# A one-core decoder layer: the token table laid out by rank, the norm passes moved behind the last low part, and the output projection's constants loaded on the pool queue

## The chip, the cores and the metric

The kernel runs on one core of a Trainium2 chip. The metric is the device time of one execution in microseconds; lower is better. A core has a matrix engine (TensorE, PE in the profile), VectorE (DVE), ScalarE (ACT), GpSimd (POOL) and SyncE (SP). Each engine works its own instructions off in order and waits for others through semaphores. DMAs are issued from the queues of SP, ACT and POOL; an issue stands in its engine's order like any other instruction, and what uses the data waits until it has landed.

## The reference

One layer over 2048 tokens of width 1024, in float32. First a mixer: one projection of the input feeds sliding-window attention, a gated linear recurrence (HGRN2) and cross-attention to 256 memory tokens; their outputs go through one output projection. Then a mixture of 16 experts of which each token uses two. Each half ends in a layer norm of a scaled residual.

```python
proj = x @ w_in[l] + b_in[l]
...
mix = jnp.concatenate([swa_with_sinks(...), hgrn2(...), memory_attention(...)], axis=-1)
x = layer_norm(ALPHA * x + mix @ w_out[l], ln1_g[l], ln1_b[l])
x = layer_norm(ALPHA * x + moe(x, w_router, router_bias, w_gate[l], w_up[l], w_down[l]), ln2_g[l], ln2_b[l])
```

The router takes, of four groups of four experts, the group whose two best scores have the largest sum, and the two best experts in it:

```python
scores = jax.nn.sigmoid((x2 @ w_router).astype(jnp.float32))
sel = scores + router_bias.astype(jnp.float32)
grouped = sel.reshape(-1, N_GROUPS, EXPERTS_PER_GROUP)
group_score = jnp.sum(lax.top_k(grouped, TOP_K)[0], axis=-1)
best = jnp.argmax(group_score, axis=-1)
...
h = jax.nn.silu(xb @ w_gate[e]) * (xb @ w_up[e])
return h @ w_down[e]
```

## The kernel before

**Precision.** Every large product is three products of rounded parts: a high part (`AF.Copy` into float32r on ScalarE) and a low part (the rest, a subtraction on VectorE) of each factor; high by high, high by low and low by high are summed (`matmul3_steps`, line 63). So each operand tile costs one ScalarE and one VectorE pass. In what follows, the split of a tile is this pair.

**Order of the work.** TensorE's instructions run in program order (`manual_schedule`). For the other engines a planner orders the instructions ahead of time: it simulates the kernel and, when an engine is free, takes the earliest in program order of those that it holds ready. `tc.issue_after` keeps an instruction behind another in that order; `hold` makes a DMA wait for another instruction. On the chip each engine then follows the planned order, whatever is ready.

**Stages.** Attention, then the recurrence (`hgrn_phase`), then the output projection with first layer norm and router (`outproj_phase`), then the experts (`moe_phase`).

**Output projection.** It goes over 16 blocks of 128 tokens. `load_mix` brings the mixer's output back from DRAM (`mixT`, written from the tile `hmix` at line 900) and splits it (lines 944 and 945). `layer_norm` normalises a block with ln1's constants `g1` and `b1`; the result goes to DRAM twice, as `x1` and as the start of the sum `z`. `g1`, `b1`, the router's weights `wr` and its bias `rb` are loaded at the head of the phase on ScalarE's queue (lines 1045 to 1054). `route_block` chooses two experts per token, some forty small VectorE operations. `rank_block` counts, by a product with a triangle of ones, how many earlier tokens chose the same expert (the rank), and scatters a pair (token, weight) of 8 bytes into a DRAM table, at row `expert * 2304 + rank`. There are two such tables, `T[0]` for the first and `T[1]` for the second choice; a row is filled in one of them only, and `fill_tables` sets all the rest to a large number in the recurrence.

**Into the experts.** `plan_slots` sorts the experts by their count of tokens: slot 0 has the fullest expert and room for 336 tokens, slots 10 to 15 have room for 256 (`CAPS`). `fetch` loads slot 0's rows of both tables (line 1500) and takes the smaller (line 1502); the token list `ig` drives the gather of the rows of `x1` into `xg` (`gathered`, line 1491). `fetch_all` loads all slots' rows of both tables in six DMAs of 8-byte elements on ScalarE's queue (line 1516), takes the smaller, and picks each slot's expert by a product with a one-hot and a sum (lines 1517 to 1530). `early` (line 1769) is a copy of slot 0's weights for `keep_warm`, twelve products whose result nobody uses, which TensorE does while it waits; then come slot 0's transposes (line 1543) and their splits (line 1545, tile `xt`).

**A slot.** `gemm1` goes over four column groups `j` of the expert's width. In each it loads and splits gate and up weights (lines 1621, 1629 and 1630), multiplies (tile `ph`), takes silu on ScalarE (1635), the product with up on VectorE (1640), and splits the result into `h` (1651 and 1652; the last line is the low part). The down weights are split in between (1606 and 1607). `gemm2` multiplies `h` by the down weights (line 1688, tile `py`) with the transposes of the next slot's tokens interleaved, scales by the router's weight, and adds the rows into `z` in DRAM (line 1725).

**The second layer norm.** As soon as a block of tokens is complete (`READY` says how many blocks are after each slot), `bring` gathers its rows of `z` (line 1563, tile `zt`). `scale` takes the statistics (`bn_stats` at 1572, `bn_aggr` at 1574) and the root, by `pow` on POOL (1582). `write` makes two VectorE passes over the block, 1586 and 1587, the first of which subtracts the mean and multiplies by `g2`, the second multiplies by the root and adds `b2`. `put` stores it (1592). `beside(j)` places these in the next slot's `gemm1`: `scale` after the first column group, `write` and `put` after the second; the last column group's product waits for the passes (`passed`). The blocks of slots 9 to 15 are 2, 1, 2, 1, 2, 2 and 2. Three more blocks follow in the ending, beside the last slot's `gemm2`; the last slot's own rows are finished where they are (1700 and 1701), and the ending takes roots by `Ln` and `Exp` on ScalarE (1578 and 1579).

A last part, for tokens that fit no slot (`plan_over`), is run only if a slot overflows.

## Time and profile before

| | us |
|---|---|
| median of 3 runs | 1642.01 |
| the three runs | 1643.66, 1642.01, 1641.55 |
| the profiled execution | 1645.28 |
| its span, first to last instruction | 1643.7 |

| engine | busy us | share of the span |
|---|---|---|
| TensorE products (PE) | 1512.4 | 92% |
| TensorE weight loads (PEld) | 1354.3 | 82% |
| VectorE (DVE) | 1144.8 | 70% |
| ScalarE (ACT) | 824.3 | 50% |
| GpSimd (POOL) | 548.7 | 33% |

A timeline row gives the start and the length in microseconds, engine, source line, operation, output and inputs, shapes, count, and in brackets how long the engine had been idle and what ended that. A `q` after the engine marks its queue, as in an issue of a DMA. A row of waits gives who waited for whom, the sum, how many times, and the longest. A row of a group gives busy time and mean ns of one. A row by stretches gives the stretch and its length, then busy time of PE, PEld, DVE, ACT and POOL with the count of instructions, then TensorE's granted clock as a share of full speed, the mean busy share of the 16 DMA engines, and GB/s. The granted clock over the whole span is 0.974.

### The profile page before, as it was taken

To read this page: it belongs to the slowest core of one execution; us is meant where nothing else is said; L and a number is where in the kernel's file an instruction comes from. 1 tells how busy PE (TensorE), PEld (TensorE's weight loads), DVE (VectorE), ACT (ScalarE), POOL (GpSimd) and SP (SyncE) were. 2 spreads that over 40 slices of the span, in tenths; PEclk is the share of its full clock that TensorE was granted. 3 is DMA by queue.
4 is the path that set the end of the run, shared out by engine and by line. 5 is a ranking of instruction groups with operands and counts; after the bars stand their busy time and mean duration, and the time that the engine had idled before them with its cause. 6 is when DMAs were issued, how large, how long until landed. Compare 5 with 4: busy or idle time off the path is not lost. (4 is left out here: it accounts for less than half of the span.)

```text
span 1643.7 us, 28391 instructions
## 1 busy us (share of the span) xinstructions
PE 1512.4 (92%) x10293; PEld 1354.3 (82%) x10293; DVE 1144.8 (70%) x2724; ACT 824.3 (50%) x1840; POOL 548.7 (33%) x723
## 2 busy tenths in 40 slices
PE   8899999978999998989999299999999999999994
PEld 7899999977899997767777188988888888989883
DVE  5688888897677678668888465554555556666667
ACT  4576776766344445343332154545555554545544
POOL 3233333465745554123333211111111124232342
PEclk9999999999999999999999699999999999999997
DMA  9422222341222222364331787777777778889872
GB/s 275 159 91 97 97 97 97 110 147 52 93 76 66 65 66 90 97 213 167 142 142 78 156 242 196 181 195 208 207 206 194 207 221 238 255 248 272 228 223 100
DMA packets 241580, 258.66 MB, mean 157 GB/s; under 512 B 26224, under 2 KB 191249, under 8 KB 241436
## 3 DMA queue, kind: packets, MB, share of 16 engines
q1 hardware_dynamic: 203216, 182.03, 35.4%
q0 software_dynamic: 21088, 69.86, 15.6%
q10 hardware_dynamic: 17132, 4.91, 1.4%
q8 instruction: 83, 1.36, 0.4%
q14 instruction: 61, 0.50, 0.1%
HBM read 189.32 MB, written 69.01 MB: 157 GB/s over the span
## 5 line engine op out<-in xcount | busy, mean ns | idle before, releaser
L63 PEld LDWEIGHTS ph<-xt,w 128*128 128x128 f32 x3072 | 394.9, 188 | 5.6 <-DVE w L1630 3.8
L63 PE MATMUL ph<-xt,w 128*128 128x256 f32 (+8 forms) x3072 | 397.1, 291 | 2.5 <-DVE w L1630 2.5
L63 PE MATMUL pj<-xt,w 128*128 128x256 f32 x2016 | 290.3, 288 | 10.0 <-DVE xt L139 4.0
L63 PEld LDWEIGHTS pj<-xt,w 128*128 128x128 f32 x2016 | 259.2, 191 | 15.9 <-DVE xt L139 5.4
L1688 PE MATMUL py<-w,h 128*128 128x512 f32 (+8 forms) x936 | 244.2, 406 | 13.3 <-DVE h L1652 12.2
L1630 DVE TENSOR_TENSOR w<-raw,w 128x1024 fp32r<-128x1024 f32 x128 | 153.2, 1221 | 85.7 <-ACT w L1629 85.5
L1688 PEld LDWEIGHTS py<-w,h 128*128 128x128 f32 (+8 forms) x936 | 161.7, 181 | 58.6 <-DVE h L1652 14.7
L63 PE MATMUL py<-w,xt 128*128 128x512 f32 x672 | 174.2, 408 | 6.8 <-ACT xt L944 6.8
L1725 POOL DMA_INDIRECT zd<-z,ioall x37 | 57.3, 1550 | 322.3 <-ACT xt L1545 213.9
L1629 ACT ACTIVATE w<-raw 128x1024 fp32r<-128x1024 f32 x128 | 132.3, 1053 | 59.9 <-PE ph L63 42.9
L63 PEld LDWEIGHTS py<-w,xt 128*128 128x128 f32 x672 | 123.7, 192 | 34.9 <-ACT xt L944 7.3
L1545 DVE TENSOR_TENSOR xt<-tr,xt 128x512 fp32r<-128x512 f32 (+8 forms) x84 | 50.3, 599 | 124.6 <-ACT xt L1545 124.4
L63 PE MATMUL pj<-w,xt 128*128 128x512 f32 x336 | 89.2, 405 | 0.0
L339 POOL TENSOR_SCALAR prob<-prob,den 128x128 f32<-128x128 f32 x128 | 45.8, 376 | 107.8 <-ACT prob L382 57.9
L1545 ACT ACTIVATE xt<-tr 128x512 fp32r<-128x512 f32 (+8 forms) x84 | 43.7, 521 | 70.1 <-PE tr L1543 70.1
L1635 ACT ACTIVATE sl<-ph 128x256 f32<-128x256 f32 (+8 forms) x64 | 25.7, 402 | 98.4 <-PE ph L63 98.4
L1607 DVE TENSOR_TENSOR w<-raw,w 128x2048 fp32r<-128x2048 f32 x32 | 73.2, 2288 | 0.0
L814 DVE COPY_PREDICATED A<-mask,pl 128x512 f32<-128x512 uint8 x56 | 50.3, 899 | 32.5 <-PE pl L812 31.5
L1239 POOL DMA_INDIRECT T<-row,dst x32 | 34.1, 1067 | 111.6 <-DVE dst L1237 95.3
L63 PEld LDWEIGHTS pj<-w,xt 128*128 128x128 f32 x336 | 60.6, 191 | 10.6
L1703 ACT ACTIVATE z<-py,tball 128x512 f32<-128x512 f32 x56 | 38.5, 688 | 55.2 <-PE py L1688 53.8
L1592 POOL DMA_INDIRECT out<-zt,fin x15 | 39.1, 2606 | 67.5 <-DVE zt L1587 65.7
(388 smaller groups left out, 2880.5 us busy)
## 6 DMA issues: line engine op xcount, KB each, us to landing
raw<-in_w_gate SPq DMA_DIRECT2D x64, 512.0 KB, 4.9
raw<-in_w_up SPq DMA_DIRECT2D x64, 512.0 KB, 5.8
raw<-in_w_down SPq DMA_DIRECT2D x32, 1024.0 KB, 8.1
xd<-xt SPq DMA_DIRECT2D x32, 512.0 KB, 6.7
xr<-in_x SPq DMA_DIRECT2D x14, 1024.0 KB, 6.2
xt<-xd POOLq DMA_DIRECT2D x20, 512.0 KB, 4.8
raw<-mixT SPq DMA_DIRECT2D x16, 512.0 KB, 4.1
x1d<-x SPq DMA_DIRECT2D x16, 512.0 KB, 2.6
```

Source lines behind the costliest of these rows:

```text
L63: nc.tensor.matmul(ps, lhsT=a, rhs=b, start=i == 0, stop=i == len(steps) - 1)
L339: nc.gpsimd.tensor_scalar(prob[:, h], prob[:, h], den[:, h:h + 1], 1.0, op0=OP.mult, op1=OP.mult)
L814: c.level = nc.vector.copy_predicated(A.rearrange("p c h (n u i) -> p (c h n) u i", u=2, i=h)[:, :, 1], mask[:, l].rearrange("p m (n i) -> ...
L1239: nc.gpsimd.indirect_dma_start(out=c.T[j][:, :], out_offset=bass.IndirectOffsetOnAxis(ap=dst[:, j:j + 1], axis=0), in_=row[:, j], in_offse ...
L1545: f["last"] = nc.scalar.activation(hi, pt, AF.Copy), v.tensor_tensor(out=lo, in0=pt, in1=f32(hi), op=OP.subtract)
L1592: return nc.gpsimd.indirect_dma_start(out=ov[n % NOUT], out_offset=indirect(t["idx"]), in_=o, in_offset=None)
L1607: v.tensor_tensor(out=t[:, 1], in0=raw, in1=f32(t[:, 0]), op=OP.subtract)
L1629: nc.scalar.activation(t[:, 0], raw, AF.Copy)
L1630: v.tensor_tensor(out=t[:, 1], in0=raw, in1=f32(t[:, 0]), op=OP.subtract)
L1688: nc.tensor.matmul(pys[hf][:m], lhsT=lhs, rhs=rhs, start=k == 0 and i == 0, stop=k == 3 and i == len(steps[k]) - 1)
L1703: nc.scalar.activation(z[:r, hs], py[:r], AF.Copy, scale=weight)
L1725: add = nc.gpsimd.indirect_dma_start(out=zv[n], out_offset=at, in_=z[:r], in_offset=None, bounds_check=S - 1, oob_is_err=False, compute_op ...
```

## The change

Four things change.

1. The token table. One table `P` replaces `T[0]` and `T[1]`. A pair with rank `128 n + p` for expert `e` goes to row `p * 272 + 16 n + e`, so that one partition's pairs of all experts and the first three rank chunks lie side by side. `table_row` works that address out with four VectorE operations. `tables` loads all slots' pairs in one DMA on ScalarE's queue (384 bytes per partition) and builds the one-hot; `of_slots` picks slots out of it, slot 0 first, and slots 1 to 15 after slot 0's last transposes have been split. The scatters write through separate views of the table. `fetch` is left for the overflow part alone. The choice of the group in `route_block` is rewritten with sums of pairs.
2. The second norm's passes. `write` is split into `centre` and `shift`. After the first column group only the first block is centred; the rest (`passes`) comes after the last low part of `gemm1`, in the last slot after the third column group. The wait `passed` goes. The gathers of the next blocks are issued after the roots on POOL. ln2's constants are loaded in slot 2 instead of slot 0.
3. The ending. One table of functions with both `Ln` and `Exp` is loaded after the last low part; the second and third block's statistics are taken on ScalarE by sums (`sums_of`).
4. The output projection's constants `g1`, `b1`, `wr` and `rb` are loaded on POOL's queue, and the small fills go to POOL.

```diff
@@ hgrn_phase
-            if 2 <= g < 4:
-                load = fill_tables(c, pad, g - 2)
+            if g == 2:
+                load = fill_tables(c, pad)
@@ outproj_phase
-        nc.scalar.dma_start(g1, a["ln1_g"].to_broadcast([128, D]))
-        nc.scalar.dma_start(b1, a["ln1_b"].to_broadcast([128, D]))
+        nc.gpsimd.dma_start(g1, a["ln1_g"].to_broadcast([128, D]))
+        nc.gpsimd.dma_start(b1, a["ln1_b"].to_broadcast([128, D]))
...
-        nc.scalar.dma_start(wr[:, :, :NE], a["w_router"].rearrange("(k p) e -> p k e", p=128))
+        nc.gpsimd.dma_start(wr[:, :, :NE], a["w_router"].rearrange("(k p) e -> p k e", p=128))
-        nc.scalar.dma_start(rb, a["router_bias"][None, :].to_broadcast([128, NE]))
+        nc.gpsimd.dma_start(rb, a["router_bias"][None, :].to_broadcast([128, NE]))
@@ rank_block
-    v.scalar_tensor_tensor(dst, idx, float(EROWS), rank, op0=OP.mult, op1=OP.add)
+    table_row(c, dst, rank, idx, ge, n, place, 2)
     for j in range(2):
-        nc.gpsimd.indirect_dma_start(out=c.T[j][:, :], ...)
+        nc.gpsimd.indirect_dma_start(out=c.pv[2 * blk + j], ...)
+def table_row(c, dst, rank, expert, ge, n, place, m):
+    v = c.nc.vector
+    v.tensor_tensor(out=ge, in0=rank[:, :, None].to_broadcast([128, m, NCK - 1]),
+                    in1=c.steps[:, None, :].to_broadcast([128, m, NCK - 1]), op=OP.is_ge)
+    v.scalar_tensor_tensor(place, rank, float(ROWS), expert, op0=OP.mult, op1=OP.add)
+    v.tensor_reduce(out=n, in_=ge, axis=AX.X, op=OP.add)
+    v.scalar_tensor_tensor(dst, n, float(NE - 128 * ROWS), place, op0=OP.mult, op1=OP.add)
@@ moe_phase
+        def tables(eos):
+            tab = cst.tile([128, NCH, NE, 2], F32, name="tab")
+            c.tabled = nc.scalar.dma_start(tab, c.P.rearrange("(p n e) w -> p n e w", p=128, n=NCK)[:, :NCH])
+            hot = cst.tile([128, NE, NE], BF16, name="hot")
+            v.tensor_tensor(out=hot, in0=eos[:, :, None].to_broadcast([128, NE, NE]),
+                            in1=c.iota16[:, None, :].to_broadcast([128, NE, NE]), op=OP.is_equal)
+            return tab, hot
+        def of_slots(tab, hot, s0, m, big):
...
+            for w in range(2):
+                t = big(NCH * m).rearrange("p (n s) e -> p n s e", n=NCH)
+                v.tensor_tensor(out=t, in0=tab[:, :, :, w][:, :, None, :].to_broadcast([128, NCH, m, NE]),
+                                in1=hot[:, None, s0:s0 + m, :].to_broadcast([128, NCH, m, NE]), op=OP.mult)
+                v.tensor_reduce(out=tb[:, w], in_=t, axis=AX.X, op=OP.add)
+                if w == 0:
+                    v.tensor_scalar(ig, tb[:, 0], float(S - 1), None, op0=OP.min)
+            c.listed = v.tensor_copy(io, tb[:, 0])
+        def sums_of(t, late):
+            z, junk = t["z"], w1p.tile([128, KC, 128], F32, name="raw1").rearrange("p k n -> p (k n)")
+            act, m = nc.scalar.activation, sm.tile([128, 4], F32, name="sums", bufs=2)
+            act(junk, z, AF.Identity, accum_out=m[:, 0:1])
+            act(m[:, 1:2], m[:, 0:1], AF.Copy, scale=-1.0 / D)
+            act(junk, z, AF.Square, bias=m[:, 1:2], accum_out=m[:, 2:3])
...
+            act(t["rs"], m[:, 2:3], AF.Ln, scale=1.0 / D, bias=eps2)
+            act(t["rs"], t["rs"], AF.Exp, scale=-0.5)
@@ gemm1
-                        if j and first:
-                            after(order, *f["last"])
+                        if first:
+                            after(order, *(f["last"] if j else (c.tabled, c.listed)))
...
-                with ExitStack() as order:
-                    if j == 3 and "passed" in f:
-                        after(order, f["passed"])
-                    mul = v.tensor_tensor(out=sl, in0=sl, in1=ps[1], op=OP.mult)
+                mul = v.tensor_tensor(out=sl, in0=sl, in1=ps[1], op=OP.mult)
@@ the loop over the slots
+            tab, hot = tables(r.eos)
+            slots = of_slots(tab, hot, 0, 1, big)
...
-                    if j == 1:
-                        for t in brought:
-                            f["passed"] = write(t, t["z"])
-                            stores.append(put(t, t["z"], len(stores)))
+                        for t in brought[:1]:
+                            centre(t, t["z"])
+                    if j == 2 and last:
+                        passes()
+                def passes():
+                    for n, t in enumerate(brought):
+                        if n:
+                            centre(t, t["z"])
+                        shift(t, t["z"])
+                        stores.append(put(t, t["z"], len(stores)))
                 gemm1(f, E[s], CAPS[s], s == 0, late, beside)
+                if not last:
+                    with ExitStack() as order:
+                        after(order, f["low"])
+                        passes()
                 with ExitStack() as order:
                     if s == 0:
-                        slots = fetch_all(r.eos, big)
+                        after(order, *f["last"])
+                        slots = of_slots(tab, hot, 1, NE - 1, big)
                         nxt = start(1)
...
+                    after(order, *(t["root"] for t in brought))
                     brought = [bring(idx=c.fin[:, b:b + 1]) for b in range(...)]
                 if last:
                     with ExitStack() as order:
-                        after(order, f["low"])
+                        after(order, f["low"], f["silu"])
+                        nc.scalar.preload_act_table_set("natural_log_exp_and_others")
+                        for n, t in enumerate(brought):
+                            (sums_of if n else scale)(t, late=True)
                         for t in brought:
-                            scale(t, late=True)
                             write(t, t["z"])
                             stores.append(put(t, t["z"], len(stores)))
```

125 lines of the change are left out of this document (60 added, 65 removed).

## The prediction

> **What bounds the kernel now.** I read the page's 40 slices first, then who TensorE waited for, then the timeline at those waits. TensorE is busy nine tenths of nearly every slice, but for one at 58% of the span:
>
> ```profile
> PE   8899999978999998989999299999999999999994
> ```
>
> So the change is worth what it takes from TensorE's own waits, and from the ending. The waits, longest in total first:
>
> ```profile
> PE py L77 <- ACT early L1769: 16.9, 1, 16.9
> PE py L1688 <- DVE h L1652: 12.2, 6, 2.6
> PE tr L1543 <- DVE xt L1545: 7.2, 1, 7.2
> PE py L63 <- ACT xt L944: 6.8, 1, 6.8
> ```
>
> The first and third are the step from the router into the first expert slot, the second lies in the late slots, the fourth at the start of the output projection. The change touches all four places. The timeline of the step into the experts:
>
> ```profile
> 916.76 0.96 POOL L1239 DMA_INDIRECT T<-row,dst  x1 [0.30 <-issue]
> ...
> 919.78 0.37 SPq L1621 DMA_DIRECT2D raw<-in_w_gate  x1
> ...
> 921.74 11.45 ACTq L1516 DMA_DIRECT2D zt<-T  x3
> ...
> 923.67 0.17 DVE L1502 TENSOR_TENSOR tb<-tab 128x6 f32<-128x6 f32 x1 [6.10 <-DMA tab<-T]
> 923.87 0.17 DVE L1504 TENSOR_SCALAR ig<-tb 128x3 int32<-128x3 f32 x1
> ...
> 924.83 1.00 POOL L1491 DMA_INDIRECT xg<-x1d,ig  x1 [7.11 <-issue]
> ...
> 933.24 0.31 ACT L1769 ACTIVATE early<-tb 128x128 bf16<-128x128 f32 x1 [16.13 <-DMA zt<-T]
> ...
> 933.60 4.73 PE L77 MATMUL py<-ones,early 128*128 128x512 bf16 x12 [16.89 <-ACT early L1769]
> ...
> 941.49 2.98 DVE L1524 TENSOR_TENSOR zt<-zt,m 128x768 f32<-128x768 f32 x2
> ...
> 946.84 0.79 PE L1543 MATMUL tr<-ident,xg 80*128 80x80 f32 x4 [7.21 <-DVE xt L1545]
> ...
> 951.02 23.01 PE L63 MATMUL ph<-xt,w 128*128 128x336 f32 x146
> ```
>
> Two things hold TensorE here. ScalarE's queue is taken by the six loads of the whole table (elements of 8 bytes, L1516) until 933.2, so `early`, TensorE's first work, comes 9 us after the list that it needs (L1502 at 923.67). Then VectorE, in order, does the 16-slot selection (from L1517 on, its first product at 941.49) ahead of the split of the first transposes.
>
> **The change part by part.**
>
> *Token table by rank: the step into the experts.* One load of 384 contiguous bytes per partition takes the place of two small loads and of six loads of the whole table; slot 0's list is picked by two products and two reductions over 48 elements; the other 15 slots' selection is ordered behind the last transpose's split. What stays in the chain:
>
> ```profile
> DMA to landing us min/median/max: 2.1/2.6/5.0
> ...
> DMA to landing us min/median/max: 3.7/3.7/3.7
> ...
> DMA to landing us min/median/max: 4.2/6.8/11.5
> ```
>
> These are, from issue to landing, the scatters (L1239), the small loads (L1500) and the gathers (L1491). The last scatter is issued at 916.76 and lands at 919.4. The new load's time is not in the trace: between the shortest small transfer (2.1) and L1500's 3.7, which shared the engines with 8-byte elements; I take 3.0, so 922.4. Product, reduction and minimum are three operations of about 0.2 where two stood, and from the end of L1504 to the first gather pass 924.83 - 924.04 = 0.8: the gather starts at 923.8. Each gather's issue holds POOL for 1.0 and 0.3 passes to the next, so the third goes at 926.4; with the 8-byte elements gone I take a landing near the low end, 4.6: 931.0. `early` needs only the list, so the 12 warming matmuls run from about 924.4 to 929.1, and the first two transposes fit before 931. From the third transpose to the first product the rows give 951.02 - 946.84 = 4.2, hence 935.2 in place of 951.0: 15.8 saved. I keep 15.0, since the array may start the slot cold. Ends: scatter 5.0, load 3.7, gathers as slow as their median leave 10.7; load 2.1 and gather 4.2 give 17.1.
>
> What is late next? Weights: slot 0's first pair is issued on SP at 919.78, behind the table loads that go away, and its second pair waits for the last gather both before and after; it then has 8 us until it is needed. VectorE's 16-slot selection, 3.0 us of products (L1524) and some 2 of reductions, now lies beside slot 0's first products (23 us of TensorE work before its first break). I cost both at nothing; if the selection went ahead of the second pair's splits, it would cost up to 2.
>
> *Norm passes behind the last low part.* One row per slot, 8 to 14; the columns that matter are the stretch and PE's busy time:
>
> ```profile
> 1304.97:1346.55 41.58, 41.58 (x297) 36.70 (x296) 21.68 (x31) 21.92 (x33) 8.11 (x7) 1.00 0.76 221
> 1346.55:1391.15 44.60, 41.73 (x273) 36.65 (x272) 28.35 (x40) 22.30 (x31) 17.85 (x12) 0.96 0.82 237
> ...
> 1427.88:1468.54 40.66, 37.67 (x257) 34.48 (x256) 26.73 (x34) 19.21 (x26) 16.14 (x9) 0.96 0.86 254
> 1468.54:1505.24 36.70, 35.84 (x257) 33.22 (x256) 22.96 (x28) 19.26 (x26) 8.69 (x8) 1.00 0.91 261
> 1505.24:1544.34 39.10, 36.07 (x257) 33.24 (x256) 26.64 (x34) 19.20 (x26) 14.51 (x8) 1.00 0.88 262
> 1544.34:1585.03 40.70, 37.67 (x257) 34.48 (x256) 26.73 (x34) 19.20 (x26) 14.63 (x8) 0.96 0.85 241
> ```
>
> Slot 8 normalises nothing and has no idle time. Slots 9, 11, 13 and 14 normalise two blocks each, 10 (left out) and 12 one. Against 41.58 for slot 9 and slot 12's busy 35.84 for the others, the excess is 3.02 + 0.86 + 4.82 + 0.86 + 3.26 + 4.86 = 17.7 us, slot 10 taken like slot 12. In three of them the granted clock is 0.96: a half-clock spell follows the gap, and it accounts for the 1.83 by which PE's busy time grows in slots 11 and 14 (37.67 - 35.84). Why TensorE waits, in slot 14:
>
> ```profile
> 1568.40 3.49 DVE L1630 TENSOR_TENSOR w<-raw,w 128x1024 fp32r<-128x1024 f32 x3
> 1571.81 0.42 DVE L1652 TENSOR_TENSOR h<-sl,h 128x256 fp32r<-128x256 f32 x1
> ```
>
> The low part that the second product's ninth matmul needs (L1652) is late, by the passes that VectorE did before these lines. After the change one pass (1.28 like L1587's 1.29 below) stays in the slot's first product and three (3.84) come behind the last low part; with one block, one and one. With 3.84 less ahead of it the low part is ready at about 1568, TensorE needs it at 1569.7: the gap closes. What is queued behind the passes instead: the splits of the next slot's transposes. The last low part would end near 1569.4, the passes at 1573.2, the first split at 1574; TensorE asks for that buffer with its third transpose; by the order of its work, 24 products of a quarter us and two transposes of 0.6 after the slot's second product begins near 1567.7, that is 1574.9. It just fits. The second thing that comes due: at 0.86 x 40.66 the transfers keep the 16 engines busy for 35.0 us of a slot that would take 35.8. I leave 1.0 us in each of the four two-block slots for these: 17.7 - 4.0 = 13.7 saved. Ends: 17.7; and nothing, if all 4 x 3.84 + 2 x 1.28 = 17.9 us of moved passes show up as waits. The pow results now come ahead of the next gathers on POOL; those gathers are used a slot later, 20 us away. The loads of ln2's constants, moved two slots, are first used in slot 9: nothing. Slot 15 does all its passes within the first product, as before, three of them later: nothing.
>
> *The ending.* After the last low part VectorE works almost without a break until the last store (the first row is a ScalarE pass of 1024 elements elsewhere, the last two are groups of the ending):
>
> ```profile
> 644.16 1.06 ACT L761 ACTIVATE sg<-e 128x1024 f32<-128x1024 f32 x1
> ...
> 1610.45 0.42 DVE L1652 TENSOR_TENSOR h<-sl,h 128x256 fp32r<-128x256 f32 x1 [0.49 <-ACT h L1651]
> ...
> 1614.36 0.20 DVE L1574 BATCH_NORM_AGGREGATE mv<-st 128x2 f32<-128x12 f32 x1
> ...
> 1631.29 1.29 DVE L1587 SCALAR_TENSOR_TENSOR z<-z,rs,b 128x1024 f32<-128x1024 f32 x1 [0.56 <-ACTq L1822]
> ...
> L1578 ACT ACT_TABLE_LOAD x5 | 6.4, 1283 | 4.3 <-DVE mv L1574 4.2
> ...
> L1572 DVE BATCH_NORM_STATS2 st<-zt 128x6 f32<-128x512 f32 x6 | 3.7, 681 | 0.0
> ```
>
> Four of these six statistics (3.7 / 6 = 0.6 each) and two of the aggregations go to ScalarE: 2.4 + 0.4, and the wait of 0.56 for the last root goes with the table loads, five at this line alone: 3.4 saved. ScalarE gets two blocks of two 1024-wide passes, 1.06 each by the same width elsewhere, with their sums and roots some 3.4 us a block, and loses the loads, so it keeps up. Ends: 0, if VectorE waits for those sums; 4.5, if TensorE's last products come earlier too.
>
> *Output projection's constants on the pool queue.* ScalarE's queue there, when TensorE next needs the norm's result, what such a store and such a constant take from issue to landing, and the transfers from 703 to 713:
>
> ```profile
> 706.01 3.15 ACTq L1054 DMA_DIRECT2D rb<-in_router_bias  x1
> 709.98 1.15 ACT L944 ACTIVATE xt<-raw 128x512 fp32r<-128x512 f32 x2 [7.02 <-DMA mixT<-hmix]
> ...
> 715.44 0.83 DVE L1166 TENSOR_TENSOR x<-x,g 128x640 f32<-128x640 f32 x1 [0.92 <-ACT x L1165]
> ...
> 724.06 0.60 PE L1109 MATMUL tr<-ident,x 128*128 128x128 f32 x4
> ...
> mixT<-hmix ACTq DMA_DIRECT2D x8, 256.0 KB, 2.1
> g<-in_ln_g ACTq DMA_DIRECT2D x2, 512.0 KB, 7.4
> ...
> DMA packets 2026, 2.47 MB, mean 247 GB/s; under 512 B 1249, under 2 KB 1505, under 8 KB 2025
> ```
>
> The four issues end at 709.16, but ScalarE's split waits until 709.96 for the store of hmix to land, whose space it takes over. Freeing the queue thus frees nothing by itself. The constants were behind that store in the same queue; on POOL they may run beside it. Two of 512 KB at the 247 GB/s of these 10 us are 4.2 us, the worst end; the best is the median 2.1 of such a store in place of 7.0, a gain of 4.9. Nearest is the present order with some sharing: I take 1.0 lost. The first norm starts at 715.4 and its block is transposed at 724.1, so a later arrival by 3 or 4 us is covered; if not, it costs what exceeds that.
>
> The Trainium skill, DMA: Bandwidth & Descriptors, section Queues, rings and completion order, says that each DMA engine goes round robin between the queues that have work. By that the 1 MB takes turns with the store, and this term would be 2 to 4 lost in place of 1.0. The row of 7.02, with the constants behind the store, cannot show it.
>
> *The router.* Eight small operations become five, and one address operation becomes four: within 0.4 either way. One table fill instead of two, and the longer overflow plan, lie beside TensorE work in stretches without waits: nothing.
>
> Sum: -15.0 - 13.7 - 3.4 + 1.0 = -31.1. The profiled execution took 1645.28 (span 1643.7), so 1614.2 for it; the median of the runs, 1642.01, is 3.27 lower, so 1611.
>
> **The rivals.**
>
> *Late slots keep their waits.* VectorE's order is set by a planner; if the next slot's splits (L1630 x3) stay ahead of the low part and wait for weights, and transfers fill the slot as computed above, the term is about 3.7, what two of the half-clock spells cost, instead of 13.7: 1621. For it: the 35.0 of 35.8. Against: slot 12, at a share of 0.91, loses only 0.86.
>
> *The half-clock spells stay.* The gaps were 2.6 us, and of four such gaps one (slot 13, clock 1.00) brought no spell. If a spell comes from something else than these gaps, 2 x 1.83 stays: 1615. Against: slots 8 and 12, without such a gap, have 1.00. The Trainium skill, TensorE: Matmul & The Clock Gate, section Why this matters for your kernels, wants idle gaps kept below about 3 us; by it the 2.6 are too short to throttle the array, and the clock rows of slots 9, 11 and 14 don't bear that out.
>
> *Slower.* The place is the second product of each slot: VectorE does the passes before the transposes' splits, both transpose buffers stay full, and TensorE stands. Full price 3.84 plus a half-clock spell of 1.83 in four slots, 1.28 + 1.83 in two: 28.9, and with nothing of the 17.7 gained, 1642 - 15.0 - 3.4 + 1.0 + 28.9 = 1653. It decides the sign from 17.4, or 2.9 us in each of six slots. Against: the first split has 0.7 us to spare by the times above.
>
> *The step into the experts gains only 10*, its low end, with the gathers at their median: 1616.
>
> *The store of hmix takes turns with the constants*, and TensorE starts the output projection 4.2 later instead of 1.0: 1614. For it: the split waits for that store. Against: 256 KB are few beside what lies ahead of them.
>
> **How the numbers follow.** Forecast (all terms near their values): 0.55. Waits kept 0.16, spells 0.08, slow gathers 0.10, the store 0.06, slower 0.05. The likeliest is 1611. The range holds the forecast, spells, gathers and waits kept, with the good ends of the step and the slots (2 + 4) and of the store (5) below: 1600 to 1626. A measurement tells 0.2%, 3.3 us, from no change; every case but the last is faster by far more: faster 0.94, same 0.02, slower 0.04.
>
> **What would show it.** Right: `early` near 924 and the first product near 935 to 937; no wait on L1652 above 1 us, granted clock 1.00 in slots 9 to 14, stretches near 36 to 37; one table load in the ending, and a last pass about 18 us after the last low part. Wrong: waits of transposes for L1545 in the second products, waits for weights in slots 11 to 14, or a gap at the output projection's start well above 7.

## The result and the profile after

| | before | after |
|---|---|---|
| median of 4 runs, us | 1642.84 | 1606.30 |
| lowest to highest | 1641.55 to 1646.30 | 1604.21 to 1608.93 |
| the profiled execution | 1645.28 | 1604.71 |
| its span | 1643.7 | 1603.1 |
| granted clock | 0.974 | 0.982 |

The ratio is 0.9775 [0.9752, 0.9799]: 36.5 us by the medians. The two profiled executions lie 40.6 apart, since that of before was 2.4 above its median and that of after 1.6 below.

The page of the changed kernel, TensorE's 40 slices, and then its list of waits, those at the places of the change (who for whom, sum, times, longest):

```profile
PE   8899999987999999899999599999999999999994
```

```profile
PE py L77 <- ACT early L1801: 7.9, 1, 7.9
...
PE py L1718 <- ACT h L1681: 2.4, 1, 2.4
...
PE py L63 <- ACT xt L944: 2.0, 1, 2.0
PE pr L1125 <- ACT rT L1120: 1.8, 2, 1.6
```

The dent at 58% of the span is half as deep in what it costs: the wait for `early` went from 16.9 to 7.9, that for slot 0's split (7.2) became one of 2.4 for the gather (below), and the 12.2 on the low part of `h` in the late slots is gone. One wait on a high part of `h` (L1681) is new.

How far the same TensorE instruction moved between the two traces, stretch by stretch:

| stretch | forecast | measured |
|---|---|---|
| attention and recurrence, to 687 us | 0 | -1.4 |
| output projection and router | +1.0 | -3.3 |
| step into the experts, with slot 0 | -15.0 | -13.7 |
| slots 1 to 8 | 0 | -0.2 |
| slots 9 to 14 | -13.7 | -20.3 |
| slot 15 | 0 | +2.6 |
| behind the last product | -3.4 | -4.3 |
| sum | -31.1 | -40.6 |

The first row is put down to chance: TensorE's work there is the same, beside one table fill instead of two, and before had a half-clock spell in the recurrence that after had not. The wait ahead of that spell was 3.0 in before and 2.5 in after, and both lengths occur in kernels with the same recurrence (last section). The step into the experts, in the changed kernel's timeline:

```profile
912.65 0.97 POOL L1241 DMA_INDIRECT P<-row,dst  x1 [0.30 <-issue]
...
916.39 0.33 ACTq L1525 DMA_DIRECT2D tab<-P  x1
...
918.77 0.33 DVE L1538 TENSOR_TENSOR zt<-tab,hot 128x48 f32<-128x48 f32 x2 [6.06 <-DMA tab<-P]
...
919.84 5.19 PE L77 MATMUL py<-ones,early 128*128 128x512 bf16 x12 [7.92 <-ACT early L1801]
...
923.06 0.90 POOL L1506 DMA_INDIRECT xg<-x1d,ig  x1 [0.30 <-issue]
...
928.38 1.11 PE L1557 MATMUL tr<-ident,xg 128*128 128x128 f32 x4 [2.40 <-DMA xg<-x1d,ig]
...
928.95 0.38 SPq L1654 DMA_DIRECT2D raw<-in_w_gate  x1
...
933.66 2.51 PE L63 MATMUL ph<-xt,w 128*128 128x336 f32 x14
```

From the last scatter's issue to the first product 34.3 us (916.76 to 951.02) became 21.0 (912.65 to 933.66). Each link can be read: the scatter 3.7 to the load's issue, the load 2.4 to its landing, 4.3 from there to the third gather's issue, 5.9 to its landing (SP's weight load, which is held for this gather, follows at 928.95), 4.7 to the first product. TensorE's wait of 2.40 is for the second gather, which was issued at 921.80 and took 6.6.

The slots 9 to 14, by stretches as the prediction's table has them, and slot 15:

```profile
1327.96:1367.81 39.85, 39.85 (x273) 35.53 (x272) 28.13 (x40) 21.99 (x30) 15.79 (x12) 1.00 0.84 247
...
1439.34:1474.95 35.61, 35.61 (x257) 33.31 (x256) 23.13 (x28) 19.22 (x26) 11.87 (x9) 1.00 1.00 295
...
1546.19:1584.77 38.58, 35.89 (x241) 32.19 (x239) 28.32 (x38) 18.29 (x34) 14.90 (x10) 0.96 0.50 148
```

These are slots 9, 12 and 15. In slots 9 to 14 the stretch equals PE's busy time to 0.1 us, at a granted clock of 1.00 in all: TensorE hardly waits. Slot 12's transfers are busy all the time (1.00), and it costs nothing. Slot 15 waits 2.7 us, at 0.96. Why, in its timeline:

```profile
1570.38 1.06 ACT L1602 ACTIVATE raw<-zt 128x1024 f32<-128x1024 f32 x1 [2.37 <-DMA zt<-zd,fin]
...
1574.06 1.13 ACT L1604 ACTIVATE raw<-zt,sums 128x1024 f32<-128x1024 f32 x1
1575.19 0.40 ACT L1681 ACTIVATE h<-sl 128x256 fp32r<-128x256 f32 x1
...
1575.64 2.04 PE L1718 MATMUL py<-w,h 128*128 128x512 f32 x6 [2.42 <-ACT h L1681]
```

ScalarE takes the sums of the two blocks, after a wait of 2.37 for their gather, ahead of the last high part of `h`, which TensorE needs. The change orders the sums behind the last low part and the silu. In the trace they and the table load come behind the silu, but ahead of the last high part (1575.19) and of the low part, which VectorE makes from it (1575.62): the low part is VectorE's, and naming it did not hold ScalarE's queue.

At the head of the output projection the order of the transfers turned round. Before (timeline, then the queues from 704 to 706 with packets, MB and share of the engines' time) the second load of rows (L955, 1 MB) was issued ahead of the store of hmix, and for two microseconds its queue moved nearly all the data:

```profile
701.99 0.37 SPq L955 DMA_DIRECT2D xr<-in_x  x1
702.99 0.37 ACTq L900 DMA_DIRECT2D mixT<-hmix  x1
```

```profile
q1 hardware_dynamic: 158, 0.64, 94.8%
```

After, the store goes first and that load behind it:

```profile
701.58 0.37 ACTq L900 DMA_DIRECT2D mixT<-hmix  x1
...
703.74 3.24 ACT L944 ACTIVATE xt<-raw 128x512 fp32r<-128x512 f32 x6 [2.20 <-DMA mixT<-hmix]
703.75 0.37 SPq L955 DMA_DIRECT2D xr<-in_x  x1
...
711.07 2.58 POOL L1168 TENSOR_TENSOR x<-x,g 128x384 f32<-128x384 f32 x2 [4.27 <-DMA g<-in_ln_g]
```

The store lands 2.2 after its issue in place of 7.0, and TensorE's wait falls from 6.8 to 2.0. With those 4.8 goes the half-clock spell behind the wait of before (granted clock 0.52 from 710.6 to 716), another 1.9. The constants now share the engines with the rows, so `g1` is late for the first norm (711.07), and TensorE gives back 3.9 of these 6.8 at the router: waits of 0.8 and 1.6 (L1120), and a half-clock spell behind them (0.72 from 721 to 727).

### The profile page after: what moved, and what is told of

Its sections match the earlier page's. It is cut to its first block, busy times and chain, and to the rows that moved or that the text cites. A ratio compares the mean times of both kernels' runs of the same rounds, so it can differ in the third digit from the quotient of the medians.

```text
span 1603.1 us, 28371 instructions
## 1 busy us (share of the span) xinstructions
PE 1507.3 (94%) x10293; PEld 1349.4 (84%) x10293; DVE 1146.9 (72%) x2721; ACT 817.4 (51%) x1843; POOL 556.1 (35%) x732
## 3 DMA queue, kind: packets, MB, share of 16 engines
q0 software_dynamic: 21472, 71.00, 16.0%
## 5 line engine op out<-in xcount | busy, mean ns | idle before, releaser
L1718 PE MATMUL py<-w,h 128*128 128x512 f32 (+8 forms) x936 | 240.6, 403 | 2.7 <-ACT h L1681 2.4
L1755 POOL DMA_INDIRECT zd<-z,io x40 | 63.7, 1594 | 282.6 <-ACT xt L1559 210.1
L63 PEld LDWEIGHTS py<-w,xt 128*128 128x128 f32 x672 | 121.9, 190 | 30.7 <-issue 4.4
L1733 ACT ACTIVATE z<-py,tb 128x512 f32<-128x512 f32 (+1 forms) x62 | 42.7, 689 | 61.2 <-PE py L1718 53.6
L1241 POOL DMA_INDIRECT P<-row,dst x32 | 34.9, 1090 | 100.1 <-DVE dst L1252 89.9
L1639 ACT ACTIVATE w<-raw 128x2048 fp32r<-128x2048 f32 x32 | 61.1, 1909 | 0.0
```

The costliest lines, as they stand in the source:

```text
L63: nc.tensor.matmul(ps, lhsT=a, rhs=b, start=i == 0, stop=i == len(steps) - 1)
L1241: nc.gpsimd.indirect_dma_start(out=c.pv[2 * blk + j], out_offset=bass.IndirectOffsetOnAxis(ap=dst[:, j:j + 1], axis=0), in_=row[:, j], in_ ...
L1639: nc.scalar.activation(t[:, 0], raw, AF.Copy)
L1718: nc.tensor.matmul(pys[hf][:m], lhsT=lhs, rhs=rhs, start=k == 0 and i == 0, stop=k == 3 and i == len(steps[k]) - 1)
L1733: nc.scalar.activation(z[:r, hs], py[:r], AF.Copy, scale=weight)
L1755: add = nc.gpsimd.indirect_dma_start(out=zv[n], out_offset=at, in_=z[:r], in_offset=None, bounds_check=S - 1, oob_is_err=False, compute_op ...
```

## Experiments: each part by itself

**The norm passes alone**, in the kernel before; with them go the order of the gathers behind the roots and the later load of ln2's constants. Table, ending and output projection stay.

```diff
-                        for t in brought:
-                            f["passed"] = write(t, t["z"])
-                            stores.append(put(t, t["z"], len(stores)))
+                        for t in brought[:1]:
+                            centre(t, t["z"])
+                    if j == 2 and last:
+                        passes()
...
+                if not last:
+                    with ExitStack() as order:
+                        after(order, f["low"])
+                        passes()
```

> The kernel before, with only the norm passes moved (and the gathers behind the roots, and ln2's constants in slot 2). Theory: slots 9 to 14 fall by what they fell in the changed kernel, from 238.5 to some 218 us (-20), because they lose their waits and the half-clock spells behind them; the last slot stays at 36.0, because its new wait of 2.4 us in the changed kernel belongs to the sums on ScalarE; the ending from the last low part to the last pass stays at 21.7. Time about 1642 - 20 = 1622. Rival 1: the last slot's wait belongs to the passes after its third column group; then it is 38.6 long here too, and the time is 1625. Rival 2: a third of the gain in the late slots came from the other parts (fewer packets in flight); then the slots fall by 13.7 as forecast, and the time is 1628.

1621.28, ratio 0.9878 [0.9863, 0.9892]: 20.9 less by the medians. Slots 9 to 14 of before, of this kernel and of the changed one, each as one stretch (three answers of the same view):

```profile
1346.55:1585.03 238.48, 224.85 (x1553) 205.31 (x1552) 155.05 (x199) 119.50 (x162) 81.45 (x53) 0.98 0.87 251
```

```profile
1340.69:1559.37 218.68, 217.93 (x1553) 201.83 (x1552) 155.10 (x199) 119.18 (x162) 78.78 (x53) 1.00 0.90 266
```

```profile
1327.96:1546.19 218.23, 218.15 (x1554) 201.98 (x1552) 154.69 (x199) 119.21 (x162) 78.97 (x53) 1.00 0.89 266
```

With the passes alone 12.9 of waits go, and 6.9 of TensorE's busy time, most of it the half-clock spells; with the whole change 13.6 and 6.7. The run does not tell the moved passes from the dropped wait `passed` or the new order of the gathers. Slot 15 has no new wait here (it is 0.7 shorter), so the 2.6 lost there belongs to the new ending. In slot 13 of this execution TensorE waits 0.75 for a transpose's split: the place that the prediction named for "slower", at a fifth of its price.

**The token table alone**, with the new way to choose the group and the new address; passes, ending and constants as before.

```diff
-                slots = fetch_all(r.eos, big)
+            tab, hot = tables(r.eos)
+            slots = of_slots(tab, hot, 0, 1, big)
...
+                        after(order, *f["last"])
+                        slots = of_slots(tab, hot, 1, NE - 1, big)
```

> The kernel before, with only the token table (and the router's group choice that came with it). Theory: from the last scatter's issue to slot 0's first product 21.0 us in place of 34.3, and 0.9 in slot 0, -14; and besides, since this version lays out the memory in such a way that the second load of rows on SP waits for the store of hmix, that store lands soon and ScalarE's split at the head of the output projection waits some 2 to 4 us in place of 7.0: -3. Time about 1625. Rival: what the output projection gained came from the constants' move to POOL; then the split waits 7 here too, and the time is 1628.

1632.38, ratio 0.9940 [0.9926, 0.9954]: 9.8 less, 7 short of the theory and 4 short of the rival. The first product of slot 0 comes 17.6 earlier than before, as meant; slot 0 then gives 4.4 back. Its timeline:

```profile
934.85 0.34 ACTq L1824 DMA_DIRECT2D g<-in_ln_g  x1
935.22 0.44 ACTq L1825 DMA_DIRECT2D b<-in_ln_b  x1
...
957.90 1.06 ACT L1656 ACTIVATE w<-raw 128x1024 fp32r<-128x1024 f32 x1 [9.45 <-DMA raw<-in_w_gate]
959.00 0.58 PE L63 MATMUL ph<-xt,w 128*128 128x336 f32 x2 [2.92 <-ACT w L1656]
```

ln2's constants, which this kernel still loads in slot 0, go out beside the weights that slot 0 now needs sooner; the weights are late by 2.92, VectorE's half of their split by 0.7, and a half-clock spell follows, 4.4 together. The prediction put the later load of those constants at nothing. Whether that is the cause was tried next.

**The token table with ln2's constants in slot 2.**

```diff
-                        nc.scalar.dma_start(g2, a["ln2_g"].to_broadcast([128, D]))
-                        nc.scalar.dma_start(b2, a["ln2_b"].to_broadcast([128, D]))
                     else:
                         after(order, f["mul"])
+                        if s == 2:
+                            nc.scalar.dma_start(g2, a["ln2_g"].to_broadcast([128, D]))
+                            nc.scalar.dma_start(b2, a["ln2_b"].to_broadcast([128, D]))
```

> The kernel before with the token table, as run already, and besides ln2's two constants (1 MB) loaded in slot 2 instead of slot 0. Theory: with the table alone slot 0 starts 13 us sooner, and those loads stand between it and its third pair of weights: waits of 2.9 and 0.7 us in slot 0 and a half-clock spell, 4.5 together. Without them slot 0 has no such wait, and the time falls from 1632.4 to about 1628. Rival: the late weights come from the 15 slots' selection on VectorE or the gathers of slot 1; then the waits stay, and so does the time, 1632.

1631.81, ratio 0.9931 [0.9910, 0.9952], which can't be told from the run before it. The two waits are gone, so they were the constants' doing; but a new one of 2.1 stands in the second product, and slot 0 still gives 2.2 back:

```profile
942.99 0.95 POOL L1506 DMA_INDIRECT xg<-x1d,ig  x1 [16.34 <-DVE io L1543]
...
946.68 7.94 SPq L1648 DMA_DIRECT2D raw<-in_w_up  x1
```

SP's issue of a weight load takes 7.94 while the gathers of slots 1 and 2 run, and the 16 DMA engines have a share of 1.04 to 1.10 from 935 to 963 us. So slot 0 has no room left for its transfers, and taking 1 MB out of it moved the wait on; that the gathers cause the new wait was not tried. Half of the theory holds.

**The constants on the pool queue alone.**

```diff
-        nc.scalar.dma_start(g1, a["ln1_g"].to_broadcast([128, D]))
+        nc.gpsimd.dma_start(g1, a["ln1_g"].to_broadcast([128, D]))
 ... (b1, wr and rb likewise; the fills of wr and eps go to POOL)
```

> The kernel before, with only the four constants and the small fills on POOL. Theory: the second load of rows (1 MB on SP, issued at about 702) still goes ahead of the store of hmix; the store lands when that load's packets are through, about 707.5 in place of 709.96: TensorE's wait falls from 6.8 to some 4.5, and part of it is given back where the first norm waits for the constants. Time 1640 to 1642. Rival: the constants behind the store, in its own queue, were what held it; then the wait falls to 2.0 as in the changed kernel, and the time is 1637 to 1638.

1642.89, ratio 1.0010 [1.0001, 1.0019]: 0.7 more by the medians, 1.6 by the ratio. The wait for the split is 7.8, longer than either theory had it:

```profile
702.78 0.37 SPq L955 DMA_DIRECT2D xr<-in_x  x1
704.16 0.37 ACTq L900 DMA_DIRECT2D mixT<-hmix  x1
...
711.95 1.15 ACT L944 ACTIVATE xt<-raw 128x512 fp32r<-128x512 f32 x2 [7.81 <-DMA mixT<-hmix]
```

The load of rows still stands ahead of the store. So the part alone costs about the 1.0 that the prediction took, and most of the 4.8 of the whole change comes from the order of rows and store (next section).

By the medians the three parts alone sum to -20.9 - 9.8 + 0.7 = -30.0 of the 36.5. The 6.5 that are missing come with the constants. The changed kernel with these back on ScalarE's queue (next section) is 28.5 faster than before, where passes and table alone sum to 30.7; the move that gains nothing by itself is worth 6.6 there.

## Experiments: the head of the output projection

**The kernel before, with the second load of rows held behind the store of hmix.**

```diff
-            XR[g] = load_rows(c, g, xp)
+            XR[g] = load_rows(c, g, xp, c.mixed if g == 2 else None)
```

> The kernel before, with the constants on ScalarE's queue, and only the second load of rows (1 MB on SP) held until the store of hmix has landed. Theory: that load ahead of the store is the larger part of the wait; the store lands 2.1 to 4 us after its issue at about 703 in place of 7.0, TensorE's wait falls from 6.8 to 2 to 4, and the time is 1638 to 1640. Rival: the constants in the store's own queue hold it; then the wait stays at 6 to 7, and the time at 1642.

1639.35, ratio 0.9982 [0.9972, 0.9993]: 2.8 less. The wait is 3.5:

```profile
703.82 0.37 SPq L955 DMA_DIRECT2D xr<-in_x  x1
704.47 0.59 ACTq L1054 DMA_DIRECT2D rb<-in_router_bias  x1
705.11 2.19 ACT L944 ACTIVATE xt<-raw 128x512 fp32r<-128x512 f32 x4 [3.70 <-DVE mv L1152]
```

The cause is shown: the 1 MB of rows made the store late. In all five profiles in which the rows went first the store landed 0.7 to 1.0 us behind them, whenever they landed. And the row says what comes due next. The split now starts when ScalarE's queue is through its four constants, the last of them issued at 704.47; the store has landed by then.

**The changed kernel with the constants back on ScalarE's queue.**

```diff
-        nc.gpsimd.dma_start(g1, a["ln1_g"].to_broadcast([128, D]))
+        nc.scalar.dma_start(g1, a["ln1_g"].to_broadcast([128, D]))
 ... (b1, wr and rb likewise; the fills of wr and eps back to VectorE)
```

> The changed kernel, with the output projection's constants and small fills back on ScalarE's queue and VectorE. Theory: the move to POOL was worth little, since the wait at the head of the output projection fell because the second load of rows there waits for the store of hmix; with the constants behind the store, TensorE's wait grows from 2.0 to some 3.6, as it was with only the rows held, and the waits of 0.8 and 1.6 us for the first norm's transposes shrink, since the constants come sooner in that queue: within 2 us of 1606. Rival: the move to POOL brought the 4.8 us; then the wait is 7 again, and the time 1610 or more.

1612.85, ratio 0.9827 [0.9810, 0.9844], 6.6 above the changed kernel by the medians. The wait of TensorE for the split is what the theory said, 3.6, 1.6 more than the 2.0 of the changed kernel. The time isn't: of the 8.1 between the two profiled executions, 1.6 is this wait, and 0.8 comes back at the router, as the theory had it; 2.8 lies in POOL's end. The rest, 2.1 in the recurrence, 0.9 in slot 14 and 1.7 more behind the last product, was not traced to the edit. POOL's end is one reason why the constants' move is worth 6.6 here and cost one alone: its last DRAIN (explained below) went from 6.85 to 7.75 us with the move alone, and goes from 6.94 to 4.12 with it in the changed kernel, by the same 352 packets.

## Experiments: the ending

**The changed kernel without the sums on ScalarE**, the table load kept.

```diff
-                            (sums_of if n else scale)(t, late=True)
+                            scale(t, late=True)
```

> The changed kernel, with the second and third block's statistics in the ending on VectorE again, and the one table load kept. Theory: the wait for the last high part goes here too (2.6 gained), and VectorE has four statistics and two aggregations more, 2.8, on its way to the last store: no change within 1.5 us of 1606. That is, the sums on ScalarE are worth nothing as they stand. Rival: the wait is not theirs; then only the 2.8 are lost, 1609.

1605.31, ratio 0.9775 [0.9762, 0.9789], the same as the changed kernel. From the last low part to the last pass VectorE takes 21.2 here and 18.7 with the sums; but slot 15 is 3.3 shorter here, so what the sums save there they cost in slot 15.

**The sums behind the last high part.**

```diff
-                        after(order, f["low"], f["silu"])
+                        after(order, f["low"], f["silu"], f["high"])
```

> The changed kernel, with the table load and the two blocks' sums in the ending ordered behind ScalarE's last high part as well. Theory: in the changed kernel the sums stand ahead of that high part in ScalarE's order, 4.7 us of work, and make the 2.4 us wait and the half-clock spell behind it; here the high part comes at 1570.5 by that trace, the wait goes, and the last slot up to the last matmul falls from 38.6 to some 35.9. VectorE's 18.7 us from the last low part to the last pass start 4 to 5 earlier, but the passes of the last rows wait for TensorE: 2.5 to 4 faster than the changed kernel, about 1603. Rival: the passes behind the last slot's third column group make the wait; then it stays, and so does the time, 1606.

1606.23, ratio 0.9785 [0.9770, 0.9801]; the same again, where 1603 was expected. The wait is gone and the last product comes 3.1 earlier, but the end only 0.8:

```profile
1572.04 0.42 DVE L1682 TENSOR_TENSOR h<-sl,h 128x256 fp32r<-128x256 f32 x1 [0.48 <-ACT h L1681]
...
1591.32 1.28 DVE L1620 SCALAR_TENSOR_TENSOR z<-z,rs,b 128x1024 f32<-128x1024 f32 x1
```

From the low part's end to the last pass's end are 20.1 us, VectorE's chain, which the later sums now delay, so the last pass ends 2.2 earlier. POOL's stores take the rest. The store of the third late block, here and in the changed kernel (start and time to landing, from the chains that ended last):

```profile
1587.07 4.12 DMA out<-zt,fin
```

```profile
1588.65 3.33 DMA out<-zt,fin
```

The last rows' stores are held until this one has landed, and the long DRAIN with which POOL ends (next section) begins 4.8 us behind the last pass in place of 3.4. So here the chain of stores ends last, not VectorE's. In slot 13 a wait of 1.5 for a transpose's split cost this execution another 1.7.

**Work taken off VectorE in the ending**, to try whether that chain is the bound: the last slot's blocks are normalised ahead of its first product, and the third late block's pass goes to ScalarE and POOL.

```diff
+        def beside_vector(t):
+            nc.scalar.activation(t["z"], t["z"], AF.Identity, scale=t["rs"], bias=t["nm"])
+            nc.gpsimd.tensor_tensor(out=t["z"], in0=t["z"], in1=g2, op=OP.mult)
+            nc.gpsimd.tensor_tensor(out=t["z"], in0=t["z"], in1=b2, op=OP.add)
...
-                            write(t, t["z"])
+                            beside_vector(t) if n == 2 else write(t, t["z"])
```

> The changed kernel with the sums behind the last high part, and besides less for VectorE in the last slot: the statistics and the first pass of the two blocks beside it are ordered ahead of its first products, where VectorE idles for 5.6 us, and the ending's third block is normalised by one ScalarE pass and two POOL operations in place of two VectorE passes. Theory: with the sums behind the high part TensorE ended 3 us sooner and the time stayed the same, because VectorE works without a break from the last low part to the last store; with 2.5 us less there and the last low part 1 sooner, 3 to 4 faster than the changed kernel: 1603. Rival: what ends last is the chain from the last product over its statistics, root, two passes and store, or POOL's operations slow VectorE down; then no change, 1606.

1611.44, ratio 0.9828 [0.9808, 0.9848]: slower than the changed kernel. The planner placed the last slot's norm ahead of slot 14's last low part, and TensorE waited 3.7 for that. Behind the last pass the DRAIN again begins 4.8 later, so the run does not show VectorE's chain to be the bound. And the passes that stay on VectorE became slower beside POOL's:

```profile
1586.25 2.38 POOL L1616 TENSOR_TENSOR zt<-zt,g 128x1024 f32<-128x1024 f32 x1 [1.69 <-ACT zt L1615]
...
1586.94 2.77 DVE L1628 SCALAR_TENSOR_TENSOR zt<-zt,rs,b 128x1024 f32<-128x1024 f32 x1
...
1597.78 1.28 DVE L1628 SCALAR_TENSOR_TENSOR z<-z,rs,b 128x1024 f32<-128x1024 f32 x1
```

The same pass takes 1.28 with POOL idle and 2.77 beside it; another, from 1590.96 on, took 3.48 beside POOL's second operation. The Trainium skill, GPSIMD Engine Reference, section 1. Specifications, lists POOL's SBUF interface as shared with VectorE, with contention for VectorE instructions that have two SBUF inputs; these rows agree, and give 1.5 and 2.2 us as the price of one pass.

## Experiments: what POOL does behind the last store

Both kernels end with DRAINs on POOL, and the longest (the last of ns min/median/max) differs by 2.7 us:

```profile
L1890 POOLq DRAIN  x3: 50/107/6853, 1636.0 to 1643.4; - x3
...
q0 software_dynamic: 21088, 69.86, 15.6%
```

```profile
L1939 POOLq DRAIN  x3: 46/109/4117, 1598.2 to 1602.8; - x3
...
q0 software_dynamic: 21472, 71.00, 16.0%
```

The first pair is of before, the second of after; the second line gives the packets that POOL's queue moved. The number of loads or of packets could be the cause, and loads whose data nobody uses tell them apart: five in slots 5 to 9 of the kernel before, one in slot 5 of the changed one, twelve in slots 3 to 8 of before.

```diff
+                        if 5 <= s < 10:
+                            spare = sm.tile([128, NE], F32, name="spare", bufs=1)
+                            nc.gpsimd.dma_start(spare, a["router_bias"][None, :].to_broadcast([128, NE]))
```

> The kernel before, with five loads of 8 KB more on POOL's queue, in slots 5 to 9, whose data nobody uses. Asked is what sets the length of the last DRAIN on POOL, which every engine waits for at the end: it took 6.85 us with 185 DMAs issued by POOL in the whole program, 6.93 with 186, 7.75 with 189, and 4.12 with 190 (the changed kernel and its variants with the constants on POOL). Theory: it depends on that count alone; here the count is 190, the drain takes 4.1 and everything else is as before: 2.7 faster, 1639. Rival: it depends on what the changed kernel does otherwise (its passes, its stores, its size); then the drain is 6.9 to 7.8 here, and the time 1642.

1643.88, ratio 1.0011 [1.0001, 1.0021]; the DRAIN is longer, 7.30 at 21248 packets. The count of loads is not what shortens it.

The one load (`if s == 5:`) in the changed kernel:

> The changed kernel, with one load of 8 KB more on POOL's queue, in slot 5, whose data nobody uses: 191 DMAs issued by POOL. Theory: the drain's length rises slowly with the count and falls back in steps; 4.1 to 4.4 here. Rival: it has nothing to do with the count; then it is 4.12, or jumps to 6.9.

A single execution, 1614.15: the DRAIN is 4.24 at 21504 packets. The time is long for other reasons: waits of 0.3 and 2.1 with a spell in slot 0 (4.5 us), and 0.9 each in slots 13 and 14. So what slot 0 gives back in the table's run can come back in the changed kernel too, though it loads ln2's constants in slot 2.

Twelve loads (two in each of slots 3 to 8), which bring the kernel before to the packets of after:

> The kernel before, with twelve loads of 8 KB more on POOL's queue, two in each of slots 3 to 8, whose data nobody uses. The count of DMAs does not set the length of POOL's last DRAIN (190 gave 7.30 us in the kernel before with five loads, 4.12 in the changed kernel). Against the packets moved by POOL's queue the runs lie on a saw: 21088 6.85, 21120 6.93, 21248 7.30, 21440 7.75, then 21472 4.12 and 21504 4.24. Each such load is 32 packets, so twelve make 21472. Theory: the packets set the length, and the drain takes 4.1 here, in a kernel that is otherwise the one before: the stretch from the last pass to the end 8.3 to 8.5 in place of 11.1, and the time 2.7 lower, 1639. Rival: what else is in the changed kernel sets it; then the drain goes on rising, to about 7.8, and the time is 1643.

1636.56, ratio 0.9967 [0.9950, 0.9983]:

```profile
L1893 POOLq DRAIN  x3: 46/103/4552, 1630.8 to 1635.9; - x3
...
q0 software_dynamic: 21472, 69.96, 16.1%
```

Twelve useless loads make the kernel 4.7 us faster by the medians. 2.3 of it is the DRAIN, 2.7 having been expected; in the profiled execution another 2 lies at the split of the output projection, long before the loads, whose wait was shorter by chance. Over all runs the DRAIN goes with the packets: 6.85 at 21088, 6.93 at 21120, 7.30 at 21248, 7.75 at 21440, then 4.12 and 4.55 at 21472, 4.24 at 21504. Profiles of one packet count agree to the nanosecond (three of 6853, three of 6935, four of 4117), but for the twelve loads: 4.55 against 4.12, so the packets alone do not give the length. It climbs and drops back, like the fill of something emptied in portions. What is emptied, the runs do not show.

## Why the prediction was right, and where it was not

The time lies in the range and 5 below the forecast, and part of that is luck. Slots 9 to 14 gave 6.6 more than forecast and the output projection 4.3 more, the second by a cause that the prediction did not have. The ending looks right, -4.3 for -3.4 behind the last product, but 2.7 of that is the DRAIN, which no step named; without it, slot 15 and the ending together would have cost 1.0.

**Slots 9 to 14: right in mechanism, too small.** The gap on the low part closed, and the half-clock spells went with it. -13.7 became -20.3. The 4.0 left for transposes and transfers was nearly 0 (0.75 and 1.5 in single slots of other executions), and 17.7, called the end, was no end: 41.58, slot 8's stretch, was taken for slot 9 without waits, and slot 9 measures 39.85 (1.7 more); four of the other five each gave some 0.2 more than their excess over slot 12's busy time (35.61 clean for 35.84).

**The step into the experts: right, 1.3 too large.** With slot 0, -13.7 for -15.0. The earlier half came as forecast (`early` 7.2 behind the last scatter's issue, 7.6 forecast). The scatter's way to the load's issue took 3.7 for 2.6 and the load 2.4 for 3.0. The third gather took 5.9 for 4.6, and from its landing to the first product went 4.7 for 4.2, since the second gather had made TensorE late. The 16-slot selection cost nothing, as said.

**Output projection: the step failed.** The text saw that the split waits for the store and asked only what the constants would do to it. What made the store late were the rows that SP loads ahead of it, which the prediction did not read. In the changed kernel that load comes behind the store, and the hold in the kernel before shows that this order alone shortens the wait: 3.5, where the kernels with the old tables and no hold waited 4.9 (passes alone) to 7.8. That the new table turned the order is shown: in every profile with it SP's load waits until the store has landed, in every profile without it and without the hold it does not, and with the table alone the split waits 3.7. Why it does is not shown; a reading that no run tests is that the table moves the tiles, so that the load's buffer overlaps the store's. "Freeing the queue frees nothing" holds only while the store is late; by the row of 705.11, ScalarE's queue is due next. The rule of the Trainium skill weighed there (DMA: Bandwidth & Descriptors, section Queues, rings and completion order) has each DMA engine take turns between queues. From 707 to 709 of the changed kernel they do:

```profile
q1 hardware_dynamic: 88, 0.36, 54.2%
...
q0 software_dynamic: 75, 0.31, 46.5%
```

From 704 to 706 of before they did not: SP's queue had 94.8% though the store had been issued at 702.99, or the store's packets were not yet there to take a turn.

**The later load of ln2's constants: "nothing" was wrong.** With slot 0 sooner they stand before its weights, a wait of 2.9 in the table's run. A faster step moves the demand of what follows. What the later load is worth stays open: with and without it the medians differ by 0.6, less than either run's spread, and a wait of 2.1 stands elsewhere in slot 0.

**The ending: right on VectorE, wrong in sum.** 21.7 to 18.7 from the last low part to the last pass is 3.0 of the 3.4, but that low part itself came late, VectorE idling 5.2 for its high part. The sums stand ahead of that high part on ScalarE, which cost 2.6 in slot 15; "it keeps up" was said of ScalarE's load and not of its order. The shorter DRAIN was not foreseen by any step.

**The rivals.** "Late slots keep their waits" and "the spells stay" fell by the rows of slots 9 to 14: no wait, clock 1.00, even with transfers at 1.00 in slot 12. "The spells stay" was priced at two spells, though slot 9 had a third (busy 41.73, now 39.85). "Slower" has its place, seen at 0.75 to 1.5 us in single slots. "Gains only 10" had its cause right: the gathers took 4.9, 6.6 and 5.9 us, the last two nearer to their median of 6.8 than to 4.6. The store did not take turns with the constants at a price of 4.2; with the constants on POOL alone TensorE started 0.8 later.

## What to carry over

When a stage starts earlier, look through the first microseconds behind it for transfers that were harmless because it was late: here constants that are first used some 400 us later held up slot 0's weights for 2.9 us, and with them gone slot 0 waited for something else. When an instruction waits for a transfer, read which other queue moved data in that time before asking about its own. An order that is tied to one engine's instruction says nothing about another engine's queue: the moved sums stood ahead of the very high part that ends the stage. And a part that gains nothing alone can be worth 6.6 us with the others, so take it out of the whole as well as putting it in alone.

## What was not expected of the hardware

The length of a wait alone does not settle whether a half-clock spell follows. Behind one untouched wait of the recurrence (L898), from 672 to 676 us, two kernels that both waited 2.42 us:

```profile
672.00:676.00 4.00, 4.00 (x27) 3.61 (x26) 2.78 (x5) 0.00 (x0) 0.81 (x2) 1.00 0.24 81
```

```profile
672.00:676.00 4.00, 4.00 (x16) 3.45 (x16) 0.72 (x2) 0.00 (x0) 1.40 (x2) 0.62 0.37 138
```

The first (the rows held back) stays at 1.00, the second (the constants back on ScalarE) falls to 0.62. Of the nine profiles in which this wait was 2.39 to 2.51, four stayed at 1.00 and five fell; in all five in which it was 2.97 to 2.99 the clock fell to 0.57 to 0.66. The Trainium skill, TensorE: Matmul & The Clock Gate, section What's actually happening, has the gate watch a free-running window of about 3.4 us, so that the point of change varies between runs; that fits a chance here, which no run tests. The limit of some 3 us for harmless gaps, in its section Why this matters for your kernels, does not fit: 2.4 is enough at times, and with the transposes on either side counted as idle it is 2.8.

The other two are the DRAIN of 4.1 to 7.75 us by the packets of POOL's queue, and VectorE's pass of 1.28 us that takes 2.77 or 3.48 beside an operation on POOL.
